# SwiGLU over a 256 MiB array: two-row tiles regrouped into four-row groups with one store each

## The chip, the cores and the metric

The kernel runs on one core of one Trainium2 chip. The metric is device microseconds (us) of one execution. A timing of this kernel is taken as the median of several runs. Times inside the kernel come from the profile of one execution, and are counted from the start of its span.

## The reference

```python
def setup_inputs():
    return {"x": np.random.randn(8192, 8192).astype(np.float32)}

def reference(x):
    a, b = np.split(x, 2, axis=-1)
    silu_b = b / (1 + np.exp(-b))
    return a * silu_b
```

Each row of 8192 float32 values is split in the middle: the left half `a` is multiplied by the Silu of the right half `b`. The input is 268.4 MB and is read once, the output is 134.2 MB and is written once. Per element there is one activation and one product.

## The kernel before

**Tiles.** A tile is 256 rows: 128 partitions with two consecutive rows each (`R = 2`). In the input these two rows are 64 KiB that lie together, in the output 32 KiB. There are 32 tiles, 0 to 31. Three buffers, `slot0` to `slot2`, hold 64 KiB per partition each, and tile `i` uses slot `i % 3`. A tile stays in its slot from its load to its store: ScalarE (ACT) replaces `b` by its Silu in place (`swiglu`, line 72), VectorE (DVE) writes the product over the first half of the slot (line 76), and the store (line 85) sends that half, 32 KiB per partition, to the output.

**Who issues what.** All loads (line 55) are issued by SyncE (SP). Stores are issued by ACT, except those of tiles 17, 19, 21, 23 and 25, which GpSimd (POOL) issues, and those of tiles 30 and 31, which SP issues. Each engine's instructions run in the order in which they are written: a store on ACT that waits for its product holds up the next Silu behind it.

**Order.** The schedule is written by hand (`tc.manual_schedule()`), and `follows_from_others` takes away waits that others already imply. The loads of tiles 0 to 2 are issued at the start. Then, for each tile: Silu, product, store, and the load of tile `i + 3` into the slot just stored, which waits for that store to land. So three tiles are in flight at any time, and the cycle of one slot is load, Silu, product, store.

**The ends.** Tile 0 is worked row by row; its output goes out in three stores (of 4, 12 and 16 KiB per partition), and tile 3 is loaded into slot 0 in two halves of 32 KiB. Tiles 1 and 2 are worked row by row and stored whole. From tile 3 on a tile is one Silu and one product of 128x8192. Tile 31 is loaded in two halves; its second row is worked in two pieces of 2048 columns, and its rows are stored one by one from SP.

Of the kernel before, what the change touches and what calls it, by code (L numbers as in the profile page):

```python
# [1 line left out]

# [4 lines left out]

_SILU = mybir.ActivationFunctionType.Silu


@with_exitstack
def kernel(
    ctx: ExitStack,
    tc: tile.TileContext,
    x: bass.AP,
    out: bass.AP,
):

    nc = tc.nc
    N, M = x.shape
    half = M // 2
    P = nc.NUM_PARTITIONS
    R = 2
    BUFS = 3  # L30

    xv = x.tensor.reshape([N // R, R * M]).ap()
    ov = out.tensor.reshape([N // R, R * half]).ap()
    ntiles = N // (P * R)
    last = ntiles - 1

    pool = ctx.enter_context(tc.tile_pool(name="sbuf", bufs=1))
    ctx.enter_context(tc.manual_schedule())
    slots = [pool.tile([P, R * M], x.dtype, name=f"slot{s}") for s in range(BUFS)]
    loads, gates, prods, stores = ([[] for _ in range(ntiles)] for _ in range(4))  # L40

    newest = {}

    def follows_from_others(inst, i, current, earlier):


        targets = [t for kind in current for t in kind[i]]
        targets += [t for kind in earlier for j in range(i % BUFS, i, BUFS) for t in kind[j]]
        for t in targets:
            if t is not newest.get(inst.ins.engine):  # L50
                tc.declare_no_dep(inst.ins, t.ins, reason="ordered by the other waits")
        newest[inst.ins.engine] = inst

    def load(i, c0=0, cw=R * M, free=None):
        inst = nc.sync.dma_start(  # L55
            out=slots[i % BUFS][:, c0 : c0 + cw], in_=xv[i * P : (i + 1) * P, c0 : c0 + cw]
        )
        if free:
            for t in loads[i - BUFS] + gates[i - BUFS] + prods[i - BUFS] + stores[i - BUFS]:
                if t is not free and t is not newest.get(inst.ins.engine):  # L60
                    tc.declare_no_dep(inst.ins, t.ins, reason="ordered by the other waits")
            newest[inst.ins.engine] = inst
        else:
            follows_from_others(inst, i, [], [loads, gates, prods])
        loads[i].append(inst)

    def swiglu(i, k0=0, k1=R, c0=0, cw=half, gated=None):
        rows = slots[i % BUFS].rearrange("p (k s c) -> p k s c", k=R, s=2)
        a = rows[:, k0:k1, 0, c0 : c0 + cw]
        b = rows[:, k0:k1, 1, c0 : c0 + cw]  # L70
        o = slots[i % BUFS][:, : R * half].rearrange("p (k c) -> p k c", k=R)
        gate = nc.scalar.activation(out=b, in_=b, func=_SILU)  # L72
        follows_from_others(gate, i, [], [loads, gates, prods, stores])
        if gated:
            gated()
        prod = nc.vector.tensor_mul(out=o[:, k0:k1, c0 : c0 + cw], in0=a, in1=b)  # L76
        follows_from_others(prod, i, [loads], [loads, gates, prods, stores])
        gates[i].append(gate)
        prods[i].append(prod)

    def store(i, c0=0, cw=R * half):
        eng = nc.scalar if i < last - 1 else nc.sync
        if i % 2 and ntiles // 2 <= i < ntiles // 2 + 10:
            eng = nc.gpsimd
        inst = eng.dma_start(  # L85
            out=ov[i * P : (i + 1) * P, c0 : c0 + cw], in_=slots[i % BUFS][:, c0 : c0 + cw]
        )
        follows_from_others(inst, i, [loads, gates], [loads, gates, prods, stores])
        stores[i].append(inst)

    for i in range(BUFS):
        load(i)
    for i in range(last):
        if i == 0:

            swiglu(i, 0, 1)
            swiglu(i, 1, 2, gated=lambda: [store(0, 0, half // 4), store(0, half // 4, half * 3 // 4)])
            load(BUFS, M, M, free=prods[0][-1])
            store(i, half, half)
        elif i < BUFS:  # L100
            for k in range(R):
                swiglu(i, k, k + 1)
            store(i)
        else:
            swiglu(i)
            if i == last - 1:
                swiglu(last, 0, 1)
            store(i)
        nxt = i + BUFS
        if nxt == BUFS:  # L110
            load(nxt, 0, M)
        elif nxt < last:
            load(nxt)
        elif nxt == last:
            load(last, 0, M)
            load(last, M, M)

    store(last, 0, half)
    for c0 in range(0, half, half // 2):
        swiglu(last, 1, 2, c0, half // 2)  # L120
    store(last, half, half)


# [1 line left out]
_INS = ['x']  # L125
_OUTS = [((8192, 4096), 'float32')]


# [23 lines left out]
```

## Time and profile before

| what | value |
|---|---|
| runs | median 935.39 us of 3 (935.21 to 936.92) |
| profiled execution | its span of 934.1 us is the one time recorded for it; the median of the runs lies 1.3 us above the span |
| DVE busy | 278.9 us, 37 products |
| ACT busy | 226.8 us, 37 Silus and a table load |
| POOL busy | 3.0 us |
| SP's DMA queue (q1): loads, and the last three stores | 5328 packets, 276.83 MB, 68.6% of the 16 DMA engines' span |
| ACT's DMA queue (q10): stores | 3888 packets, 104.86 MB, 26.0% |
| POOL's DMA queue (q0): five stores | 720 packets, 20.97 MB, 5.2% |
| HBM | 268.44 MB read, 134.22 MB written, 431 GB/s over the span |

One transfer of 128 partitions is spread over 16 DMA engines. The packet counts show how: 720 packets for five stores are 144 for each, which is 128 that carry one partition's run of bytes each and 16 more, one per DMA engine, of 4 bytes, which report the landing. Each DMA engine therefore moves 8 partitions of every transfer. "Share" is the time that a queue's packets took out of the time of all 16 engines. An idle compute engine costs nothing as long as these 16 have packets to move.

### The profile page before, as it was taken

What the parts mean: (1) busy time and instruction counts of PE and PEld (TensorE: products, weight loads), DVE (VectorE), ACT (ScalarE), POOL (GpSimd) and SP (SyncE); (2) the same over time, 40 slices, a digit from 0 to 9 for tenths busy, and PEclk for the clock granted to TensorE, in tenths of its full rate; (3) what the DMA queues carried; (4) which work ended last, traced back from release to release, by engine and by line L of the source; (5) the groups of instructions that cost most, each with busy time, mean ns of one, the idle gap of its engine ahead of it and who ended that gap; (6) DMA issues with size and microseconds to landing.
All of it is one profiled execution on the core that took longest, in us unless ns stands there. A gap on an engine that the chain in (4) does not pass through costs nothing.

```text
span 934.1 us, 228 instructions
## 1 busy us (share of the span) xinstructions
DVE 278.9 (30%) x37; ACT 226.8 (24%) x38; POOL 3.0 (0%) x9
## 2 busy tenths in 40 slices
DVE  0333123332133321333312333133331233312342
ACT  0431320233302333113331133311333113331141
POOL 0000000000000000000000000000000000000000
DMA  9999999999999999999999999999999999999998
GB/s 404 418 425 435 429 450 424 446 429 425 448 420 436 427 450 425 425 439 452 432 415 455 413 443 428 431 445 427 431 428 459 415 428 445 429 445 428 428 427 383
DMA packets 9937, 402.67 MB, mean 431 GB/s; under 512 B 1104, under 2 KB 1104, under 8 KB 1232
## 3 DMA queue, kind: packets, MB, share of 16 engines
q1 hardware_dynamic: 5328, 276.83, 68.6%
q10 hardware_dynamic: 3888, 104.86, 26.0%
q0 software_dynamic: 720, 20.97, 5.2%
q14 instruction: 1, 0.01, 0.0%
HBM read 268.44 MB, written 134.22 MB: 431 GB/s over the span
## 4 chain that ended last, share of the span: by engine, by line
DMA 74%; DVE 10%; ACT 7%; issue 6%; another core or an unknown queue 1%; DVEq 0%; SPq 0%; POOL 0%; ACTq 0%; POOLq 0%
DMA slot<-in_x_dram 40%; DMA out_dram<-slot 34%; DVE slot L76 10%; ACT slot L72 7%; DVEq L147 0%; SPq L55 0%; POOL out_dram L85 0%; ACTq L85 0%; DVEq L76 0%; POOLq L147 0%
## 5 line engine op out<-in xcount | busy, mean ns | idle before, releaser
L76 DVE TENSOR_TENSOR slot<-slot 128x8192 f32<-128x8192 f32 (+2 forms) x37 | 278.9, 7539 | 641.4 <-ACT slot L72 641.1
L72 ACT ACTIVATE slot<-slot 128x8192 f32<-128x8192 f32 (+2 forms) x37 | 225.5, 6105 | 690.0 <-DMA slot<-in_x_dram 690.0
L85 POOL DMA_DIRECT2D out_dram<-slot x5 | 2.8, 558 | 756.8 <-DVE slot L76 756.8
L72 ACT ACT_TABLE_LOAD x1 | 1.3, 1283 | 0.7 <-PEq L136 0.7
L136 POOL MEMSET const-bfloat16-1.0<- 128x1 bf16 x1 | 0.1, 102 | 0.0
L136 POOL MEMSET const-float32-0.0<- 128x1 f32 x1 | 0.1, 98 | 0.2 <-issue 0.2
L136 POOL MEMSET const-float32-1.0<- 128x1 f32 x1 | 0.1, 98 | 0.0
L136 POOL MEMSET const-uint8-127<- 128x1 uint8 x1 | 0.1, 98 | 0.0
## 6 DMA issues: line engine op xcount, KB each, us to landing
out_dram<-slot ACTq DMA_DIRECT2D x24, 4096.0 KB, 34.7
out_dram<-slot POOLq DMA_DIRECT2D x5, 4096.0 KB, 33.8
slot<-in_x_dram SPq DMA_DIRECT2D x4, 4096.0 KB, 29.7
out_dram<-slot SPq DMA_DIRECT2D x1, 4096.0 KB, 19.3
out_dram<-slot SPq DMA_DIRECT2D x2, 2048.0 KB, 14.5
out_dram<-slot ACTq DMA_DIRECT2D x1, 2048.0 KB, 47.0
out_dram<-slot ACTq DMA_DIRECT2D x1, 1536.0 KB, 41.8
out_dram<-slot ACTq DMA_DIRECT2D x1, 512.0 KB, 24.6
```

Of the source, the lines that this page charges most:

```text
L72: gate = nc.scalar.activation(out=b, in_=b, func=_SILU)
L76: prod = nc.vector.tensor_mul(out=o[:, k0:k1, c0 : c0 + cw], in0=a, in1=b)
L85: inst = eng.dma_start(out=ov[i * P : (i + 1) * P, c0 : c0 + cw], in_=slots[i % BUFS][:, c0 : c0 + cw])
L136: nc = _bacc.Bacc("TRN2", target_bir_lowering=False, num_devices=1)
```

## The change

Tiles 0, 1 and 2 at the beginning and tiles 29, 30 and 31 at the end stay two-row tiles. The 26 tiles between become 13 groups of 512 rows: 128 partitions with four consecutive rows each, 128 KiB of input and 64 KiB of output that lie together per partition.

- The two outer slots, `s0` and `s2`, take turns as the group's accumulator `acc`. It is loaded with the first two of the four rows; the middle slot, `side`, is loaded with the other two. Both loads have 64 KiB per partition, and the step from one partition's run to the next in HBM is now 128 KiB, where it was 64 KiB.
- The product of the first two rows is written over the first half of `acc` in one piece, as before. The other two rows are worked in four pieces of 2048 columns, whose products go from `side` into the second half of `acc`.
- One store from ACT then sends the whole of `acc`, 64 KiB per partition. Tile stores of the middle part, those of POOL among them, are gone.
- The next load of `side` no longer depends on a store. It waits for the last product and for a GpSimd `memset` of an unused buffer, `spare` (128x3072 float32), which itself starts after the last product, so "with the store". The load of `acc` for the group after next waits for the store.
- On SP the order is: `side` for group g+1, `acc` for group g+2, `side` for group g+2, and so on. On ACT: Silu of `acc` (one), Silu of `side` (four), the store. After the 13 groups, tile 29 is in `s2`, 30 in `side`, and 31 in `s0`, in two halves. Store 29 is on ACT; stores 30 and 31 are on SP.
- The bookkeeping of waits is written anew (`ordered`, `behind`); each instruction now names the waits that it keeps.

The head (loads of tiles 0 to 2, the three stores of tile 0, the halves loaded into `s0` behind them) stands in the same order as before. The core of the diff:

```diff
-    R = 2
-    BUFS = 3
+    W = 2 * M
+    HEAD = 3
+    ngroups = (ntiles - 2 * HEAD) // 2
...
+    x4 = x.tensor.reshape([N // 4, 2 * W]).ap()
+    o4 = out.tensor.reshape([N // 4, W]).ap()
...
-    slots = [pool.tile([P, R * M], x.dtype, name=f"slot{s}") for s in range(BUFS)]
+    s0, side, s2 = (pool.tile([P, W], x.dtype, name=f"slot{s}") for s in range(3))
+    spare = pool.tile([P, 3072], x.dtype, name="spare")
...
+    def four(g, part):
+        r = HEAD * P // 2 + g * P
+        return x4[r : r + P, part * W : (part + 1) * W]
...
+    def swiglu(src, dst, d0, parts, landed, gated=None):
+        s3 = src.rearrange("p (k s c) -> p k s c", k=2, s=2)
+        d3 = dst[:, d0 : d0 + M].rearrange("p (k c) -> p k c", k=2)
+        prods = []
+        for k0, k1, c0, cw in parts:
+            a = s3[:, k0:k1, 0, c0 : c0 + cw]
+            b = s3[:, k0:k1, 1, c0 : c0 + cw]
+            o = d3[:, k0:k1, c0 : c0 + cw]
+            gate = ordered(nc.scalar.activation(out=b, in_=b, func=_SILU), landed)
...
+            prods.append(ordered(nc.vector.tensor_mul(out=o, in0=a, in1=b), [gate]))
+        return prods
...
+    quarters = [(k, k + 1, c, half // 2) for k in range(2) for c in (0, half // 2)]
...
+    for g in range(ngroups):
+        acc = s2 if g % 2 else s0
+        swiglu(acc, acc, 0, whole, main[g])
+        prods = swiglu(side, acc, M, quarters, [extra])
+        r = HEAD * P // 2 + g * P
+        done = ordered(nc.scalar.dma_start(out=o4[r : r + P, :], in_=acc[:, :]), prods[-1:])
+        pause = nc.gpsimd.memset(spare[:, :], 0.0)
+        behind(pause, prods[-1], "begins with the store")
+        extra = load(side, four(g + 1, 1) if g + 1 < ngroups else two(last - 1), prods)
+        behind(extra, pause, "some time behind the store")
+        if g + 2 < ngroups:
+            main.append([load(acc, four(g + 2, 0), [done])])
+        elif g + 2 == ngroups:
+            main.append([load(acc, two(last - 2), [done])])
         else:
-            follows_from_others(inst, i, [], [loads, gates, prods])
-        loads[i].append(inst)
...
-        eng = nc.scalar if i < last - 1 else nc.sync
-        if i % 2 and ntiles // 2 <= i < ntiles // 2 + 10:
-            eng = nc.gpsimd
...
+            final = [load(acc, two(last), [done], c0, M) for c0 in (0, M)]
...
+    prods = swiglu(s2, s2, 0, whole, main[ngroups])
+    store(nc.scalar, last - 2, s2, prods)
+    prods = swiglu(side, side, 0, whole, [extra])
+    p0 = swiglu(s0, s0, 0, row0, final[:1])
+    store(nc.sync, last - 1, side, prods)
+    store(nc.sync, last, s0, p0, 0, half)
+    p1 = swiglu(s0, s0, 0, halves, final[1:])
+    store(nc.sync, last, s0, p1, half, half)
```

## The prediction, made before the changed kernel was run

> **What bounds the kernel now.** I read the page from the top: engines, then the slices of the DMA engines, then the DMA queues.
>
> ```profile
> span 934.1 us, 228 instructions
> ...
> DVE 278.9 (30%) x37; ACT 226.8 (24%) x38; POOL 3.0 (0%) x9
> ...
> DMA  9999999999999999999999999999999999999998
> ...
> q1 hardware_dynamic: 5328, 276.83, 68.6%
> q10 hardware_dynamic: 3888, 104.86, 26.0%
> q0 software_dynamic: 720, 20.97, 5.2%
> ```
>
> No compute engine is busy for a third of the span. The three queues together fill 68.6 + 26.0 + 5.2 = 99.8% of what 16 DMA engines have. This is a kernel that moves bytes without a pause. The view by stretches says where the rate is lower; columns are the stretch, its length, busy time of DVE, ACT and POOL, clock, DMA share and GB/s:
>
> ```profile
> 0.00:25.00 25.00, 0.00 (x0) 3.50 (x2) 0.20 (x4) 1.00 0.99 419
> 25.00:50.00 25.00, 12.56 (x3) 12.03 (x4) 0.00 (x0) 1.00 1.00 430
> 50.00:75.00 25.00, 10.35 (x4) 7.12 (x2) 0.00 (x0) 1.00 0.95 397
> ...
> 129.00:158.00 29.00, 8.69 (x1) 7.03 (x1) 0.00 (x0) 1.00 1.00 434
> ...
> 587.00:616.00 29.00, 8.69 (x1) 7.03 (x1) 0.00 (x0) 1.00 1.00 434
> ...
> 876.00:905.00 29.00, 8.69 (x1) 7.89 (x2) 0.00 (x0) 1.00 0.98 424
> 905.00:934.00 29.00, 8.92 (x3) 6.47 (x3) 0.00 (x0) 1.00 0.91 390
> ```
>
> The middle stands at 434 GB/s, with stores from ACT alone (129 to 158) and with POOL's among them (587 to 616). One tile moves 12.58 MB, which at 434 GB/s is 29.0 us, and 29.0 us is the period of the tiles. All 402.65 MB at 434 GB/s would take 927.8 us, so at most 934.1 - 927.8 = 6.3 us of the span are not pure transfer, and they lie in the first 75 us and the last 58, which the change leaves nearly as they are. The longest waits look large but are the other side of this:
>
> ```profile
> SPq L55 <- DMA out_dram<-slot: 832.6, 30, 37.3
> ACT slot L72 <- DMA slot<-in_x_dram: 690.0, 33, 32.6
> DVE slot L76 <- ACT slot L72: 641.1, 33, 34.1
> ```
>
> SP waits for a store before each load, yet the DMA engines had the other slots' packets meanwhile. These waits are worth nothing by themselves. What can cost time is only a moment at which a DMA engine has no packet in any queue, or packets that take longer.
>
> **The price of a packet.** The trace records each packet. In the middle all 64 KiB load packets took 2.418 us, all 32 KiB store packets 1.213 us, the 4-byte ones 0.009 us, and successive packets of one DMA engine overlap by some 0.004 us. Two queues with work take turns, packet by packet.
>
> **The change, part by part.**
>
> *Stores.* Removed: 26 tile stores of 8 packets of 32 KiB per DMA engine, 208 x 1.213 = 252.3 us. Added: 13 group stores of 8 packets of 64 KiB, priced like the 64 KiB load packet: 104 x 2.418 = 251.5 us. Difference 0.83 us; 13 fewer landing packets, 0.12 us. Without the overlap, which 117 fewer packets lose too (117 x 0.004 = 0.47 us), it is 0.48 us. So 0.5 to 0.95 us are gained on a path that is the bound; I take 0.6, nearer to the lower end, because the period of 29.0 us agrees with the packets less their overlap (8 x 2.414 + 8 x 1.209 = 28.98).
>
> *The same bytes, fewer transfers: a rule.* The row is the period: it holds the packets and nothing else, so what a transfer costs at its start and end is hidden by other packets. The Trainium skill, page "DMA: Bandwidth & Descriptors", section "Anatomy of one DMA — SWDGE (gpsimd) path", gives each transfer about 2 us of fixed cost. By that rule, paid in full, 13 fewer transfers would save 26 us (an estimate from the page), which no stretch at 434 GB/s has to give.
>
> *POOL's five stores.* They go to ACT's queue. Both stretches above have 434 GB/s, so nothing is won or lost.
>
> *Compute.* Per group the second half is worked in quarters. By form, a 128x2048 Silu is 1.902 us and a product 2.288 us, against 7.029 and 8.693 for 128x8192: 4 x 1.902 - 7.029 = 0.58 us more on ACT, 4 x 2.288 - 8.693 = 0.46 us more on DVE, 13 times. The engines are 24% and 30% busy; the cover is the 58.0 us a group's 25.17 MB take. On the slot's own cycle it is a gain: landing to store is 1.9 + 4 x 2.29 + some 0.4 for handovers = 11.5 us, instead of 15.8 (162.33 to 178.12 in the chain). Without the cover the added work would be 13 x 0.5 = 6.5 us.
>
> *Waits on ACT.* A group's store waits for the last product, some 2.4 us after ACT's last Silu. Behind it on ACT is the Silu of the next `acc`, which has not landed by then (next point), so nobody waits for that.
>
> *The memset.* The trace has GpSimd memsets of 128x1 only, 0.098 us. From below it is 0.1 us; from above, per column, a product's 8.693 us / 8192 x 3072 = 3.3 us, and a Silu's would be 2.6. I take 3 us. Queued behind it: on POOL only the next memset; on SP, behind the load of `side`, the load of `acc`, which must wait for the store's landing anyway. When the `side` load is issued, the DMA engines still hold the previous `acc` load and the store, so it costs nothing up to some 15 us.
>
> *Does a DMA engine ever run dry?* This is the decision. A 64 KiB load is 8 packets, 19.3 us alone. (1) `side` lands; from then the next `acc` load runs alone. The store is issued 11.5 us later, and its first packet comes 3.5 us or more after issue (as in rows of before: issue at 556.45, first packets 559.99 to 562.15). So 15 to 17.5 us of 19.3 are gone and one or two packets of `acc` are left. (2) The store's 8 packets take turns with load packets: one or two of `acc`, its landing packet, and five or six of `side`, whose load has been in the queue for long. (3) At the store's end two or three `side` packets remain, 4.8 us at least. The next `acc` load needs its landing seen and issued, 0.34 us (123.42 to 123.76), and 1.0 us from issue to first packet (0.98 to 1.98), plus the spread of the 16 engines' ends, since the landing counts when the slowest is done: 0.7 us at the start (21.93 to 22.65), 1.4 up to 510 us, 2.4 to 2.7 after 540. Sum 2.1 to 4.0 us against 4.8: covered, by 0.8 to 2.7 us.
>
> *The first group* has no tile store at 121.5. Loads up to tile 5 and stores up to tile 2 are 6 x 19.35 + 3 x 9.7 = 145.2 us of packets, begun at 2: enough until 147, and the group's store is issued by about 141, with first packets at 145. *The tail*: tile 29's store lies behind the last group's on ACT; tile 31's halves behind tile 30's load; SP's three stores queue behind loads on the same ring, as before. I count it at zero; its bounds are the spread of the engines' ends, 1.4 us either way.
>
> *HBM.* Load runs now step by 128 KiB instead of 64, store runs by 64 instead of 32. The nearest row: loads already step by twice what stores do and cost per byte no more (2.418 against 2 x 1.213), so I take zero. From above, the slowest stretch after the start, 397 GB/s for 434, on the 26 tiles' loads: 26 x 19.3 x 0.09 = 45 us. Against the change speaks the Trainium skill, same page, section "Latency and other measured facts": rows at a large power of two apart slow a copy, 207 GB/s at 512 KiB against 214 padded. No run here has shown that; at that page's ratio, were it to hold at 128 KiB, 26 x 19.3 x 3.4% would be 17 us (an estimate from the page).
>
> **Sum.** Span 934.1 - 0.6 = 933.5; with the 1.3 us by which the runs' median stands above the span, 934.8 us. Measurement can tell about 0.2%, 1.9 us, from no change; this is 0.06%.
>
> **The rivals.**
>
> 1. *The cover is one packet short* (slower). If the store's first packet comes one turn earlier, or the landing is seen late, one `side` packet is left, 2.4 us, against a need of 2.1 to 4.0: up to 1.6 us idle in each of 13 groups, half of that 0.8 x 13 = 10 us: 945 us. It decides where spread plus 1.4 us exceeds what is left; one store of before had a spread of 3.9 us (tile 2, 119.56 to 123.42). Against it: a leading engine that idles does not delay the slowest one.
>
> 2. *HBM steps* (slower). Packets of over 2.418 us; from a tenth of the bound, 5 us, to all of it: 940 to 980 us. Against it: in the middle every packet took the same time, whatever lay beside it.
>
> 3. *A gain that shows* (faster): the full 0.95 us and an end without the 1.4 us spread, 933.0 us. It needs both.
>
> 4. *The long stores are cut*: 64 KiB store runs travel as 32 KiB packets. Then 935.3 us, no change. Against it: load packets are 64 KiB.
>
> **How the numbers follow.** Forecast 0.68, cut stores 0.03, rival 1 0.16, rival 2 0.07, rival 3 0.06. Of rival 1 a fifth stays under 1.9 us, so the same is 0.68 + 0.03 + 0.03 = 0.74, less 0.03 for a worse tail: 0.71; slower 0.23, faster 0.06. The range: low end 933.3, near rival 3; upper end 939.5, the forecast with a third of a microsecond lost per group, which leaves out some 0.14 above and 0.05 below.
>
> **What will show it.** Right: stretches of 58 us in the middle at 434 GB/s or a shade above, queue shares that still sum to nearly 100%, q10 with 19 transfers of 144 packets, 2736 instead of 3888, 64 KiB stores landing in 40 us or more since they take turns, a period of 57.9 us from store to store. Rival 1: DMA share below 1.00 just after each store's landing, period 59 us or more. Rival 2: share at 1.00 but GB/s under 434. A memset of over 15 us would break the argument on SP.

## The result: slower by 1.5%, and the profile after

The changed kernel takes 949.74 us, median of 5 runs (948.14 to 951.0), against 935.39 before: ratio 1.0149, 95% interval 1.0138 to 1.016. The forecast was 934.8 with a range up to 939.5; the time lies beyond it. From the page of the changed kernel:

```profile
span 948.0 us, 316 instructions
...
DVE 281.5 (30%) x76; ACT 230.4 (24%) x77; POOL 34.8 (4%) x17
...
DMA  9999999999999999999999999999999999999998
...
q1 hardware_dynamic: 5328, 276.83, 68.9%
q10 hardware_dynamic: 2736, 125.83, 30.7%
...
L124 POOL MEMSET spare<- 128x3072 f32 x13 | 34.6, 2658 | 818.5 <-DVE slot L89 818.5
```

The span grew by 13.9 us, and yet the two queues fill 68.9 + 30.7 = 99.6% of the DMA engines' time. q1, the loads and the last three stores, has the same 5328 packets and 276.83 MB as before, but its share of a longer span is 653 us (0.689 x 948.0) where it was 641 (0.686 x 934.1): 12 us. The stores cost the same, 291 us on both sides. So load packets took longer, and nothing else did much. Stretches of the changed kernel, each from one group's store to the next (columns: stretch, length, busy DVE, ACT and POOL, clock, DMA share, GB/s):

```profile
141.00:199.00 58.00, 17.59 (x5) 14.34 (x5) 2.57 (x1) 1.00 1.00 434
...
258.00:317.50 59.50, 17.59 (x5) 14.34 (x5) 2.52 (x1) 1.00 0.99 422
317.50:377.00 59.50, 17.59 (x5) 14.34 (x5) 2.76 (x2) 1.00 1.00 423
...
496.00:556.00 60.00, 17.59 (x5) 14.34 (x5) 2.81 (x2) 1.00 1.00 418
...
733.50:792.00 58.50, 17.54 (x5) 14.34 (x5) 2.66 (x1) 1.00 1.00 428
```

The first period is what was forecast, 58 us at 434 GB/s. From the third to the eighth a period is 59.2 to 60.1 us, with a DMA share of 0.99 to 1.01 but only 418 to 423 GB/s; near the end it comes back to 58.6. A full share at under 434 GB/s is the sign that the prediction had set for rival 2, the HBM steps, and a period of 59 us or more is one of rival 1: the signs alone did not tell the two apart, the experiments below do. SP's waits show the new order:

```profile
SPq L69 <- DMA out_dram<-slot: 614.4, 17, 41.6
SPq L69 <- POOL spare L124: 233.8, 13, 20.4
```

The `acc` loads still wait for stores, 17 waits in all with those of the head; the 13 `side` loads wait for the memset.

**What the packets say.** In the trace's packet records I added up, after 100 us and per DMA engine, what load packets took over their usual 2.418 us (1.213 for 32 KiB), and the time without a packet. I sorted it by place: the first packet of a load; a load packet that is followed by a store packet; the rest. The records do not name the DMA engine, so I strung the packets into 16 rows, in which each starts as the one before it ends. The sums do not depend on how that is done, but the split between "first" and "other" can be off by up to half a microsecond.

| run | median us | span | first of a load | before a store packet | other | no packet | sum |
|---|---|---|---|---|---|---|---|
| before | 935.39 | 934.1 | 0.0 | 0.0 | 0.0 | 0.0 | 0.0 |
| changed | 949.74 | 948.0 | 2.0 | 9.2 | 1.3 | 1.1 | 13.6 |
| e1_no_memset | 950.7 | 946.9 | 1.7 | 8.9 | 1.3 | 0.8 | 12.7 |
| e2_tile_pitch | 978.77 | 976.6 | 8.3 | 10.3 | 0.4 | 24.2 | 43.2 |
| e3_early_half_store | 935.68 | 933.9 | 0.0 | 0.1 | 0.0 | 0.0 | 0.1 |
| e4_groups_reversed | 950.75 | 953.3 | 3.6 | 11.8 | 1.2 | 2.3 | 18.9 |
| e5_pause_x6 | 937.48 | 936.4 | 1.0 | 1.1 | 0.2 | 0.1 | 2.4 |
| e6_pause_x3 | 948.51 | 945.7 | 1.3 | 8.8 | 1.0 | 0.9 | 11.9 |
| e7_acc_in_halves | 937.31 | 935.3 | 0.0 | 0.9 | 0.1 | 0.1 | 1.1 |
| e8_late_acc | 946.41 | 943.6 | 1.6 | 6.5 | 1.2 | 0.7 | 9.9 |
| e9_pause_x4 | 940.02 | 938.6 | 0.7 | 3.4 | 0.2 | 0.4 | 4.7 |
| e10_pause_x5 | 936.56 | 934.7 | 0.4 | 0.4 | 0.0 | 0.1 | 0.9 |

The sums agree with what each span exceeds 934.1 to within 0.7 us, so the table accounts for the time. Two things happen in the changed kernel, in one group after the other. Around the third group's store (group 2, counted from 0):

- The store of group 2 is done on the first DMA engine at 298.11 and on the last at 301.36. SP issues the next `acc` load at 301.70; its first packets start from 302.93 on, just as the `side` packets end on the leading DMA engine (302.94). On the leading engines the load comes when nothing else is left, and its first packet takes up to 3.2 us.
- Some 20 us later the next store is issued at 317.43 and starts at 323.23 to 324.84. The load packet just ahead of it takes 3.5 to 3.9 us, on all 16 DMA engines.

Around the stores of groups 0 and 1, where the `acc` load came with time to spare (2.9 us or more from issue to first packet), neither is seen; just ahead of the store of group 2 single packets already reach 3.0 us, 0.13 us over the usual on average. The chain of waits up to the store of group 3, in the changed kernel:

```profile
260.55 45.99 DMA slot<-in_x_dram
306.53 0.02 issue
306.56 1.92 ACT slot L86
308.48 0.02 issue
308.50 8.91 DVE slot L89 x4
317.41 0.02 issue
317.43 0.02 POOLq L124
317.45 0.07 issue
317.51 2.67 POOL spare L124
```

### The profile page after: what moved, and what is told of

Same layout as the page of the kernel before. It is cut to its first block, busy times and chain, and to the rows that moved or that the text cites. A ratio compares the mean times of both kernels' runs of the same rounds, so it can differ in the third digit from the quotient of the medians.

```text
span 948.0 us, 316 instructions
## 1 busy us (share of the span) xinstructions
DVE 281.5 (30%) x76; ACT 230.4 (24%) x77; POOL 34.8 (4%) x17
## 3 DMA queue, kind: packets, MB, share of 16 engines
q1 hardware_dynamic: 5328, 276.83, 68.9%
q10 hardware_dynamic: 2736, 125.83, 30.7%
## 4 chain that ended last, share of the span: by engine, by line
DMA 78%; DVE 13%; POOL 3%; ACT 3%; issue 0%; DVEq 0%; SPq 0%; POOLq 0%
DMA slot<-in_x_dram 69%; DVE slot L89 13%; DMA out_dram<-slot 9%; POOL spare L124 3%; ACT slot L86 3%; DVEq L168 0%; SPq L69 0%; POOLq L124 0%; DVEq L89 0%
## 5 line engine op out<-in xcount | busy, mean ns | idle before, releaser
L89 DVE TENSOR_TENSOR slot<-slot 128x2048 f32<-128x2048 f32 (+2 forms) x76 | 281.5, 3747 | 652.7 <-ACT slot L86 652.4
L86 ACT ACTIVATE slot<-slot 128x2048 f32<-128x2048 f32 (+2 forms) x76 | 229.2, 3068 | 700.3 <-DMA slot<-in_x_dram 700.3
L124 POOL MEMSET spare<- 128x3072 f32 x13 | 34.6, 2658 | 818.5 <-DVE slot L89 818.5
```

Source lines behind the costliest of these rows:

```text
L86: gate = ordered(nc.scalar.activation(out=b, in_=b, func=_SILU), landed)
L89: prods.append(ordered(nc.vector.tensor_mul(out=o, in0=a, in1=b), [gate]))
L124: pause = nc.gpsimd.memset(spare[:, :], 0.0)
```

## The experiments

After the result I had three theories. **A**, the schedule: with one store per group, the `acc` load hangs on the store's landing, and the cover of `side` packets is too thin; loads run alone for 20 us before the next store. **B**, HBM: loads that step by 128 KiB. **C**: the memset, or the load issued behind it.

**e1: without the memset.**

```diff
-        pause = nc.gpsimd.memset(spare[:, :], 0.0)
-        behind(pause, prods[-1], "begins with the store")
...
-        behind(extra, pause, "some time behind the store")
```

> The load of the side slot waits for the last product alone; the GpSimd memset is gone. In the profile of the changed kernel the 64 KiB load packet that is under way when a group's store starts takes up to 3.9 us instead of 2.418 (9.2 us per DMA engine over the groups), and the first packets of the next acc load come late (2.0 us longer, 1.1 us idle). Theory A (the schedule: loads alone for 20 us, then a store joins; and a thin cover at the store's landing): the memset has no part in it, 948 to 951 us. Rival C (the memset, or the side load issued right behind it into the moment at which the store starts, makes that packet long): the 9.2 us vanish, about 940 us. Rival B (loads that step by 128 KiB read more slowly): 948 to 951 us.

950.7 us, 1.0133 to 1.02 times before; the long packets are all there (8.9 us). The memset is not the cause. Here the `side` load is issued together with the store, so whether its issue near the store's start matters is not settled by this run; e8 settles it.

**e2: the groups made of two old tiles.** Loads step by 64 KiB again; one store writes two runs of 32 KiB per partition.

```diff
-        return x4[r : r + P, part * W : (part + 1) * W]
+        return two(HEAD + 2 * g + part)
...
-        done = ordered(nc.scalar.dma_start(out=o4[r : r + P, :], in_=acc[:, :]), prods[-1:])
+                out=o2[r : r + 2 * P, :].rearrange("(t p) m -> p t m", t=2),
+                in_=acc[:, :].rearrange("p (t m) -> p t m", t=2),
```

> Same schedule, waits, engines and transfer counts, but a group consists of two of the old two-row tiles: every load steps by 64 KiB again, and the one store per group writes two runs of 32 KiB per partition instead of one of 64. Theory A (schedule): no change, 948 to 951 us, long load packets at the store's start still there. Rival B (the 128 KiB step of the loads, or the 64 KiB store packet, is what costs): back to 935 to 937 us and 64 KiB load packets of 2.418 us.

978.77 us, 1.0448 to 1.0479. B falls, and both expectations missed the size: it is 29 us slower still. Queues of this run, from its page:

```profile
span 976.6 us, 316 instructions
...
q1 hardware_dynamic: 5328, 276.83, 67.5%
q10 hardware_dynamic: 4400, 125.83, 29.8%
```

The shares sum to 97.3%: here the DMA engines do run dry, 24.2 us each by the records. The reason follows from the turns: a store now has 16 packets of 32 KiB, each taking a turn with a load packet of 64 KiB, and only nine (first group) to thirteen load packets are there. They are used up before the store ends, so its last one to five packets follow one another and there is no cover at its landing at all. It is what rival 1 would be with no cover, at (978.77 - 935.39) / 13 = 3.3 us a group; of these 24.2 / 13 = 1.9 us are idle time, the rest long packets.

**e3: the first half of the group's output is stored as soon as its product is there**, in a store of its own; the next `acc` load waits for both.

```diff
+        early = ordered(nc.scalar.dma_start(out=o4[r : r + P, :M], in_=acc[:, :M]), firsts)
...
-        done = ordered(nc.scalar.dma_start(out=o4[r : r + P, :], in_=acc[:, :]), prods[-1:])
+        done = ordered(nc.scalar.dma_start(out=o4[r : r + P, M:], in_=acc[:, M:]), prods[-1:])
```

> Four-row groups and 128 KiB load steps stay, but the group's output goes out in two stores of 32 KiB per partition, the first as soon as the first product is there, so that stores are spread over the period and loads do not run alone for 20 us. Theory A (schedule): 935 to 938 us. Rival B (the 128 KiB step): 948 to 951 us. If only the thin cover at the store's landing mattered and not the stretch of loads alone: in between, about 945 us.

935.68 us, 0.9993 to 1.0013: no difference from before. Two of its periods:

```profile
316.00:374.00 58.00, 17.59 (x6) 14.34 (x5) 2.66 (x1) 1.00 1.00 434
374.00:432.00 58.00, 17.59 (x6) 14.34 (x5) 2.66 (x1) 1.00 1.00 434
```

Four-row groups, 128 KiB steps and the memset are all in it. What is gone is the one long store, with its packets of 64 KiB, its stretch of loads alone and its thin cover (the `acc` loads have 7.0 us or more from issue to first packet), and with it the whole loss. Which of these it was, the next runs tell: e5 and e10 keep the 64 KiB store packets and the stretch of loads alone, and lose almost nothing.

**e4: the groups in reverse order of rows.**

```diff
-        r = HEAD * P // 2 + g * P
+        r = HEAD * P // 2 + (ngroups - 1 - g) * P
```

> The 13 groups are worked from the last rows to the first; nothing else changes. In the changed kernel's profile the long packets lie in groups 3 to 10 of 0 to 12, hardly in 0 to 2, 11 and 12. If they belong to places in HBM, the total stays near 950 us and the pattern is mirrored (long from the 2nd to the 9th in order of time, none late). If they belong to the order in time (how far the 16 DMA engines have drifted apart), 948 to 951 us with the same groups by number in time.

946.48 and 955.03 us, 1.0106 to 1.0216. There are only two runs, one on each side of the 948 to 951 us expected. By the packet records of the profiled execution, the slower of the two, the long packets lie in the `acc` loads ahead of the store of group 2 in time and of all later ones, to the last, but for group 4, whose store follows the one `acc` load in this stretch that had 3.1 us from issue to first packet. They are not mirrored: they go with the order in time, not with places in HBM. Most `acc` loads have only 1.0 to 1.6 us from issue to first packet here.

Within A a question was open. **A1**: the late `acc` load is the cause, the long packet at the store's start its consequence. **A2**: they are separate.

**e5: six memsets, 15.9 us of pause.** The `side` load then enters after the previous `acc` load has ended, the store gets turns to itself, and more `side` packets are left at its landing.

```diff
         behind(pause, prods[-1], "begins with the store")
+        for _ in range(5):
+            pause = nc.gpsimd.memset(spare[:, :], 0.0)
```

> Six memsets of 2.66 us in place of one, 15.9 us: the side load is queued after the previous acc load is done, so the store has two or three packet turns to itself, and one or two more side packets (2.4 to 4.8 us) are left when the store has landed. Theory A1 (thin cover: the acc load waits for the store's landing and comes after the side packets have run out on the leading DMA engines; the long packet at the next store's start is a consequence of that): both go, 934 to 937 us. Theory A2 (the late acc load and the long packet at the store's start are separate; the latter belongs to a store that joins loads which ran alone): only about 3 us come back, 944 to 947 us. Against any cover theory: 948 to 951 us.

937.48 us, 1.0011 to 1.0029. The store's landing is no less spread than before (347.35 to 353.91 in group 3), but from issue to first packet the `acc` loads now have 7.0 us or more. Both losses go, as A1 said. The upper end of its expectation is passed by half a microsecond: 1.0 us lies in first packets, now of the `side` load, which here enters an empty queue beside the running store. Counted in packets, the changed kernel has two `side` packets left on a DMA engine when its part of the store is done, in some groups on some engines only one (in group 3 on twelve of the 16); the run with six memsets has four to six, mostly five.

**e6, e9, e10: three, four and five memsets** (8.0, 10.6, 13.3 us), the same edit with other counts.

> Three memsets, 8.0 us. The previous acc load still has packets until some 10 to 12 us after the store's issue, and the side load queues behind it in the same queue anyway, so by the reckoning of packets the cover does not change: 947 to 951 us under A1 and A2. If the pause acts from its first microsecond on: between the changed kernel and the run with six, 940 to 945 us.

> Four memsets, 10.6 us. From the packets the side load must come later than the turn at which the previous acc load ends, 12 us or so after the store's issue, to give the store a turn of its own; at 10.6 us this is just missed on most DMA engines: 944 to 949 us. If the gain rises evenly with the pause: about 944 us between three (948.5) and six (937.5).

> Five memsets, 13.3 us: past that turn, so one more side packet is left at the landing, nearly the whole effect of six: 937 to 940 us. If the gain rises evenly with the pause: about 941 us.

948.51 (1.0126 to 1.0179), 940.02 (1.0036 to 1.007) and 936.56 us (1.0003 to 1.0022). With five, 10.6 us more of waiting in each group than in the changed kernel, which looked like pure loss, brought back 13 us of the whole time. It is a threshold and no even rise: nothing up to 8 us, nearly all at 13. At 10.6 us the result is better than the 944 to 949 us expected: that pause is near the turn at which the previous `acc` load ends, so the DMA engines split (two or three `side` packets left, with five memsets three to five). Periods with five:

```profile
200.00:258.00 58.00, 17.59 (x5) 14.34 (x5) 13.32 (x6) 1.00 1.00 434
258.00:316.00 58.00, 17.59 (x5) 14.34 (x5) 13.25 (x6) 1.00 1.00 434
```

and its chain, a group of 58.2 us from store to store:

```profile
431.80 2.67 POOL spare L124
434.47 0.05 issue
434.52 2.67 POOL spare L127
...
445.35 33.71 DMA slot<-in_x_dram
479.06 0.02 issue
479.08 1.92 ACT slot L86
481.00 0.02 issue
481.02 8.91 DVE slot L89 x4
```

The `side` load issued at 445.35 lands within 33.71 us, against 45.99 in the changed kernel's chain above: issued 11 us later after the store, it loses nothing, since it had only been queued.

**e7: the cover from the other side.** The pause is as in the changed kernel. The store is cut in two behind the last product, and the next `acc` load in two halves, the first of which waits for the first store alone.

```diff
+        done = [
+            ordered(nc.scalar.dma_start(out=o4[r : r + P, c : c + M], in_=acc[:, c : c + M]), needs)
+            for c, needs in ((0, firsts), (M, prods))
+        ]
+        behind(done[0], prods[-1], "both stores behind the last product")
...
-            main.append([load(acc, four(g + 2, 0), [done])])
+            main.append([load(acc, four(g + 2, 0), [done[c // M]], c, M) for c in (0, M)])
```

> The pause is as in the changed kernel. The group's store is cut into two of 32 KiB per partition, issued one after the other behind the last product as before, and the next acc load into two halves, of which the first waits for the first store alone. So the load queue gets its next packets while the second store still runs: the cover is made from the other side, and loads still run alone before each store. A1: 935 to 937 us (descriptors cost 1 us more than in the changed kernel). A2: 944 to 948 us.

937.31 us, 1.0011 to 1.0029, with 0.9 us of long packets. That is 0.3 us above what A1 expected. Loads still run alone before each store, and the store still starts behind the last product; what is gone is the late load. But the packets of the stores and of the `acc` loads, those just ahead of the next store among them, are 32 KiB here, so this run alone does not separate A1 from an effect of the packets' size. e8 does.

**e8: e5 with a late `acc` load**, delayed by two memsets that begin at the store's landing.

```diff
+            late = nc.gpsimd.memset(spare[:, :], 0.0)
+            behind(late, done, "begins at the landing")
+            late = nc.gpsimd.memset(spare[:, :], 0.0)
...
+            behind(main[-1][0], late, "some time behind the landing")
```

> The run with six memsets (937.5 us, hardly any long packets), but the next acc load also waits for two more memsets, 5.3 us, that begin at the store's landing. There the first acc packet came 7.0 us after the load's issue, because side packets were still left; with 5.3 us taken away the load comes as late as in the changed kernel (1.2 to 2 us from issue to first packet). If a late acc load brings the long packets at the next store's start by itself (A1): 945 to 950 us and some 8 us per DMA engine of lengthened load packets at the store's start. If the long packets had another cause that the longer pause removed (A2, for instance that the side load meets the store's start): 938 to 941 us, with only the late first packets back.

946.41 us, 1.0093 to 1.0133, as A1 said; 6.5 us of long packets at the store's start are back, a little under the 8 expected. By the records seven of the twelve delayed loads still have 2.1 to 3.2 us from issue to first packet, five 1.0 to 1.6. The `side` load is issued here as late as in e5, so its place near the store's start is not the cause: with this, theory C falls whole.

The runs can also be read load by load. For the `acc` load behind each of the first twelve groups of the changed kernel, e6, e8, e9 and e10 (60 loads), this is the shortest time from issue to first packet, and what the load packet just ahead of the next store took over 2.418 us, as a mean over the 16 DMA engines:

| issue to first packet, us | loads | excess just ahead of the next store, us: mean (range) |
|---|---|---|
| 0.95 to 1.66 | 17 | 1.07 (0.36 to 1.56) |
| 1.78 to 2.40 | 16 | 0.51 (0.14 to 1.15) |
| 2.53 to 3.22 | 11 | 0.06 (0.00 to 0.13) |
| 3.64 to 6.40 | 16 | 0.02 (0.00 to 0.09) |

That the 16 DMA engines have drifted apart does not do it by itself: in e10 the first packets of an `acc` load are up to 2.4 us apart, as in many groups of the changed kernel, and the packet ahead of the next store takes on average no more than 0.03 us over 2.418.

## Why the prediction was wrong, by its own steps

**The step that failed** is "Does a DMA engine ever run dry?". It set a need of 2.1 to 4.0 us against a cover of 4.8 and called it covered. Three things in it were wrong.

- *The spread.* I took 0.7 to 2.7 us from the rows of before. In the changed kernel the landing of the group stores spreads over 0.65 us in group 0, 1.6 in group 1 and 3.25 in group 2, and the landing counts when the slowest of 16 is done. With 0.34 + 1.0 us the need is 4.6, not 2.1 to 4.0. The kernel before had shown 3.9 us once, and I kept that for the rival. The cover itself was right in most groups, two `side` packets or 4.8 us, so by this sum even a need of 4.6 would have been covered.
- *Just in time is too late.* I compared the arrival with the end of the last `side` packet. The runs show that more is needed, and this is the step that decides. In the changed kernel itself, the `acc` load with 3.7 us from issue to first packet stands in a period of 58.1 us; those with 2.0 to 2.9 us in periods of 58.6 to 58.9; those with 1.1 to 1.6 in periods of 58.8 to 60.1. With 4.4 us and over (e10) a group loses 0.07 us. One reading is a DMA engine that settles its next packet when it starts the present one: in the rows of before, a store issued beside 64 KiB loads needs 3.5 us to its first packet, the 1.0 us of an idle queue and one packet of 2.4. It is only argued, and it does not fit well: by it a load with 2.5 to 3.2 us would still come too late, and such loads did next to no harm (0.06 us in the table above). What was measured is that the harm fades between 1.6 and 2.5 us.
- *The price.* Rival 1 was priced by idle time, 0.8 us a group. Idle time turned out to be 1.1 us in all. The larger part, 9.2 us, are packets that take longer, far from the moment at which the load was late. With 2.0 and 1.3 us of other long packets it is 13.6 / 13 = 1.05 us a group. So the rival's 945 us came near by luck as much as by insight: it named the right moment, but nearly all of its 10 us were to be idle time. Its condition was also turned round: a store that comes a turn later, not earlier, leaves one `side` packet instead of two, as on many DMA engines in groups 3 and 4. My objection that a leading engine's idling does not delay the slowest one missed that all 16 get the long packet.

**What held.** The packets: 2736 instead of 3888 on ACT's queue, and the store packets of 64 KiB took 2.418 us, as priced. The first group's period, 58.09 us. HBM at zero: in e3 the loads step by 128 KiB, and all that their packets take over 2.418 us is 0.1 us per DMA engine after the first 100 us. The rule of the Trainium skill (page "DMA: Bandwidth & Descriptors", section "Latency and other measured facts") starts at a step of 512 KiB and is not contradicted; at 128 KiB no run here shows a cost. The 2 us a transfer that the prediction quoted belong, as its section's title says, to transfers that GpSimd issues, and only five of the 26 replaced stores were such; 13 fewer transfers saved nothing that shows. The memset, 2.658 us where I took 3, costs nothing (e1), as said; that it was too short to do anything was not said. Compute in quarters: 0.6 us more on ACT and 0.5 on DVE per group, hidden. The times at which the prediction places packets (556.45 us and the like) stand 0.24 us later than the profile's own zero; their differences, which are all that it uses, hold.

**What cannot be told.** The 0.5 to 0.95 us that longer stores were to save: the run with five memsets has a span of 934.7, of which 0.9 us are lengthened packets; the 933.8 that remain are 0.3 us below before, less than executions differ.

**Open.** Why an `acc` load that comes late lengthens, some 20 us later, the load packet ahead of the next store. e5 and e8 show that the one brings the other; what a DMA engine does in between, the records do not show. A late `acc` load is not the only way to a long packet: in e5, where none is late, 1.1 us remain ahead of stores, single packets of up to 3.1 us among them. No version here beats the kernel before; the nearest are e3 (1.0003) and e10 (1.0012).

## What to carry to other kernels

Where the DMA engines are full, as here, merging transfers gained nothing that could be measured, and it concentrated the moments at which a buffer comes free. Ask for each load that waits for a store how many packets are left in the other queues when the store lands on the slowest engine, and want one packet more than the arithmetic asks for: here an issue 1.0 us before the last packet's end looked early enough, and only from 2.5 us on was the harm gone. A share of 1.00 is no proof that the engines are at full rate; compare the GB/s of the same stretch, or share times span for the same bytes. If a load has to wait anyway, delaying another one can be the cheapest way to have packets left at the right moment.

## What the runs showed of the hardware that was not expected

- A load packet of 64 KiB, 2.418 us in any mixture with stores before, took 3.5 to 3.9 us just ahead of the first packet of group 3's store, on all 16 DMA engines together (2.9 to 4.3 us in groups 3 to 8 of the changed kernel). Its store packets stayed at 2.418 us, at most 2.47.
- The first packet of a load that comes when no queue has anything left takes about 3.0 us, both at the very start of the changed kernel (2.7 to 3.4) and in the middle (the `acc` loads of e2, 3.0 to 3.2 as a mean over the 16 engines). An empty queue of its own is not enough: the `side` loads of e5 enter one beside a running store, and their first packets take 2.42 to 2.66 us on average.
- Two queues with work alternate packet by packet whatever the packets' sizes, in e2 one 32 KiB store packet and one 64 KiB load packet in turn on all 16 engines, until the loads' run out. So 16 store packets of 32 KiB use up as many turns as 16 of 64 KiB would: cutting a long store's runs in half (e2) took away its cover and cost 29 us more.
- The 16 DMA engines, 0.65 us apart after the head, drifted to 3.3 us apart by the landing of group 2's store, in the changed kernel.
